# Two transformer blocks on 256 tokens: logits by quarters of rows, a put-off residual, a transferred pair of rows and cross-attention of raw rows

## The chip, the cores and the metric

One core of one Trainium2 chip. The metric is the device time of one execution in microseconds (us); a lower time is better. The core's engines work side by side: TensorE (PE, matrix products; its weight loads are shown as PEld), VectorE (DVE), ScalarE (ACT), GpSimd (POOL) and SyncE (SP), whose queue issues the stream of weights.

## The reference

x has 256 rows of 1024 columns, in f32. Block one, once:

```
h = rms_norm(x, g_mix);  z = h @ w_in           # q, k, v, su, sv, two gates
x += (sig(ga) * (attention(q, k, v) @ w_att_out) + sig(gb) * (sgu(su, sv) @ w_sgu_out)) @ w_out
x += cross_attention(rms_norm(x, g_cross), rms_norm(mem, g_mem))   # 4 heads of 128
x += moe(rms_norm(x, g_moe))       # best of 4 groups, then top 2 of its 4 experts
x  = rms_norm(x, g_final)
```

In cross-attention the scores are softmax(q k^T / sqrt(128)) with q = h @ w_cq, and w_ckv gives keys and values of the normed memory; then @ w_co. The MoE has 16 experts of (silu(t Wg) * (t Wu)) Wd with 512 hidden columns.

Block two, twice (the mixer is stick-breaking attention, then retention), with shift, scale and gate from c:

```
x = layer_norm(sqrt(2) * x + (1 + gate) * mixer(x * (1 + scale) + shift))
x = layer_norm(sqrt(2) * x + (1 + gate) * moe2(x * (1 + scale2) + shift2))
```

Stick-breaking attention takes log(1 - sigmoid(z)) under a causal mask, its suffix sums, and weighs values with exp(log sigmoid(z) + suffix), masked. moe2 is the same kind of MoE; its groups are ranked by the sum of the two best softmax values.

## The kernel before

x lies in SBUF as two tiles of 128 rows (t = 0, 1) side by side, each of two halves of 512 columns (n = 0, 1). All weights, about 440 MB, come through SP's queue in units of 1 MB in the order of use (`Stream`, lines 97 to 207), into a ring of 22 units (RING) in 24 tiles. Dense stages split each unit into a high part (ACT, line 172) and the rest (DVE, line 173) and multiply in three products (lines 423 to 425 and 441 to 443). A planner orders each engine's instructions by program order and estimated costs; what is wrapped in `keep_in_program_order` ("pin") stays in program order.

Block one (`block1`, from line 501) ends with cross-attention. `denseT` makes ck, the keys (line 696), then `T` turns m, the merged branches, by sixteen PE transposes (line 354; ACT line 372 and DVE line 373 evict), and the output product updates x (line 705). `normed` (line 330) makes xn, x times its rows' norm factor; the products of the values cv are the filler `fill`, two steps of which run before the transposes of xn (c) and the product cq. `xscores` makes scores for each head and calls `softmax` (lines 471 to 487: maximum, Exp with the row sums, reciprocal, and two ACT copies, line 486, that divide). `probT` (line 495) transposes, and line 751 multiplies with the values.

Each MoE (`moe`, from line 976) begins with a prelude: sixteen transposes of x, evicted with the scale sc into Y by eight operations of 128x256 (lines 361 and 363); the norm's factors; warming matmuls (`warm`, line 384, products of constants that nobody reads; the WARM tuples give their numbers for the three MoEs); products with the router's weights (line 1010), a copy (line 1014) and a product that adds four partial sums (line 1016); the normed rows xs (lines 1020 to 1024); the logits lg (line 1028); `route`, a chain of small DVE operations whose result sl lets PE compute places (line 1041); more warming; then the dispatch products px (line 1188). Seven rounds follow (`ROUNDS`), each for the slots of 2 to 4 experts: gate products pg, up products pu, down products py (line 1066, 7 us each). `down` splits the weighed results (lines 1103 to 1108) and adds them to x through the placing products pc (`put`, lines 1117, 1118, 1120): the first half of the columns at once, the second half, put(1), after a `yield`, which the next round resumes once its gate products stand:

```
late = down(hid, downs, wsl[:, p % 2 : p % 2 + 1], PT, tiles(p == LAST), p, p == LAST)
next(late, None)
if p in (XP - 1, LAST):
    self.do(late)
```

XP = 4, so after the fourth round put(1) is done at once, and then comes a branch (`extras`, line 1359) around a loop for tokens that no slot took. With even p a product pw (line 1203) brings the slot weights of two rounds.

In the third MoE the gain and bias of the last norm (four rows of 512) are fetched by POOL (`gains`), and in the sixth round (HOOK = 5) `rows` spreads them over the partitions by eight products (`spread`, line 1498) with four ACT copies. `last_norm` (line 1452) has three quarters on DVE and one on ACT and POOL, then the output's four transfers. In `stick`, POOL multiplies sp with a triangle of ones (line 1568) ahead of z's products (line 1576).

## Time and profile before

| what | value |
|---|---|
| runs | 1292.48, 1294.85, 1300.04 us; median 1294.85 |
| profiled execution | 1298.88 us, of it the span 1297.3 |
| mean granted TensorE clock | 0.979 of full speed |
| busy | PE 1214.7 us, DVE 729.5, ACT 404.6, POOL 126.8 |
| moved | 445.08 MB, mean 343 GB/s |

The span reaches from the first to the last instruction. [...] Block one lasts to 240 us, its MoE to 459, stick-breaking attention to 602, the second MoE to 832, retention to 1051, the third MoE to 1286. In a timeline line, "[2.21 <-DVE m L373]" says that the engine was idle for 2.21 us before this instruction, and what released it; "x16" joins sixteen neighbours.

### The profile page before, as it was taken

How to read it: one execution, taken by the hardware profiler on the slowest of the kernel's cores; microseconds unless marked ns; L12 is line 12 of the kernel's file. 1: busy time of each engine (PE TensorE's matmuls, PEld its weight loads, DVE VectorE, ACT ScalarE, POOL GpSimd, SP SyncE). 2: the span in 40 equal slices, each digit the busy share in tenths (PEclk: the TensorE clock that was granted, in tenths of full speed). 3: DMA queues.
4: the chain of work that ended last, by engine and by line, in shares of the span. 5: the costliest groups of instructions: out<-in, count | busy, mean ns of one | idle time of the engine just before them, and what ended most of it. 6: DMA issues, size and time to landing. Idle time of an engine off the chain costs nothing. (4 is left out here: it accounts for less than half of the span.)

```text
span 1297.3 us, 18613 instructions
## 1 busy us (share of the span) xinstructions
PE 1214.7 (94%) x6985; PEld 767.9 (59%) x6985; DVE 729.5 (56%) x1621; ACT 404.6 (31%) x695; POOL 126.8 (10%) x136
## 2 busy tenths in 40 slices
PE   6999988999999889999999899799999999998995
PEld 5877867644434378876443344488888874433442
DVE  5999986622222189976633222579898653332225
ACT  5776536310000144663100001243346431000011
POOL 1000200000000021332000000230102000000101
PEclk9999998999999989999999999999999989999998
DMA  9976867699999998787799999958798577999991
GB/s 366 407 271 257 307 284 297 255 410 421 421 419 422 418 421 311 280 312 274 283 420 421 420 420 419 421 215 297 265 330 341 185 301 293 419 420 421 419 416 44
DMA packets 64352, 445.08 MB, mean 343 GB/s; under 512 B 7364, under 2 KB 7876, under 8 KB 11904
## 3 DMA queue, kind: packets, MB, share of 16 engines
q1 hardware_dynamic: 62352, 439.91, 85.1%
q10 hardware_dynamic: 1296, 2.61, 0.5%
q8 instruction: 57, 0.93, 0.3%
q0 software_dynamic: 608, 1.32, 0.3%
q14 instruction: 39, 0.32, 0.1%
HBM read 442.75 MB, written 1.05 MB: 342 GB/s over the span
## 5 line engine op out<-in xcount | busy, mean ns | idle before, releaser
L173 DVE TENSOR_TENSOR hl<-w,hl 128x1024 fp32r<-128x1024 f32 (+1 forms) x154 | 191.3, 1254 | 53.4 <-ACT hl L172 52.9
L172 ACT CAST hl<-w 128x1024 fp32r<-128x1024 f32 (+1 forms) x160 | 165.3, 1040 | 172.1 <-PE dn L425 93.9
L1066 PE MATMUL pg<-w,XT 128*64 128x512 f32 (+1 forms) x864 | 162.8, 599 | 0.0
L1066 PE MATMUL py<-w,hid 128*64 128x512 f32 (+2 forms) x912 | 155.7, 573 | 3.0 <-ACT hid L1080 3.0
L1066 PE MATMUL pu<-w,XT 128*64 128x512 f32 (+1 forms) x864 | 155.8, 603 | 0.0
L1405 DVE TENSOR_TENSOR hid<-hid,pu 128x512 f32<-128x512 f32 x21 | 14.4, 687 | 179.0 <-PE pu L1066 179.0
L1120 DVE TENSOR_TENSOR x<-x,pc 128x512 f32<-128x512 f32 (+1 forms) x90 | 54.8, 648 | 89.3 <-PE pc L1118 88.7
L1066 PEld LDWEIGHTS pu<-w,XT 128*64 128x64 f32 (+1 forms) x864 | 47.0, 126 | 95.6 <-issue 93.3
L1066 PEld LDWEIGHTS py<-w,hid 128*64 128x64 f32 (+1 forms) x912 | 48.8, 125 | 91.9 <-issue 82.3
L1066 PEld LDWEIGHTS pg<-w,XT 128*64 128x64 f32 (+1 forms) x864 | 47.3, 126 | 91.7 <-issue 90.3
L829 DVE CUSTOM_DVE_ANT_0 w<-w,scr,vec 128x512 f32<-128x512 f32 x96 | 73.0, 790 | 0.0
L829 DVE CUSTOM_DVE_ANT_0 w<-w,scr,adaT 128x512 f32<-128x512 f32 x96 | 72.7, 792 | 0.0
L1054 PE MATMUL px<-O,xs 128*128 128x128 f32 x576 | 70.5, 276 | 0.0
L1054 PEld LDWEIGHTS px<-O,xs 128*128 128x128 f32 x576 | 67.1, 192 | 2.5 <-issue 2.5
L1391 ACT ACTIVATE hid<-pg 128x512 f32<-128x512 f32 x21 | 12.6, 599 | 159.9 <-PE pg L1066 159.9
L1107 ACT CAST yh<-y 128x512 fp32r<-128x512 f32 x26 | 16.1, 620 | 126.1 <-DVE y L1106 116.5
L1058 POOL TENSOR_TENSOR XT<-XT,adaT 128x512 f32<-128x512 f32 x24 | 25.0, 1042 | 286.7 <-DVE XT L1056 217.2
L1087 ACT CAST O<-pP 128x256 fp32r<-128x256 f32 x21 | 7.8, 373 | 143.1 <-PE pP L1086 134.0
L423 PE MATMUL dn<-hl,h 128*128 128x512 f32 (+1 forms) x128 | 49.5, 392 | 2.9 <-ACT hl L172 2.9
L423 PE MATMUL dn<-hl,e 128*128 128x512 f32 x128 | 51.0, 398 | 0.0
L1106 DVE SCALAR_TENSOR_TENSOR y<-py,ws,gate 128x512 f32<-128x512 f32 x26 | 19.5, 750 | 55.3 <-PE py L1066 55.2
L425 PE MATMUL dn<-hl,e 128*128 128x512 f32 x128 | 49.9, 390 | 0.0
(541 smaller groups left out, 2319.5 us busy)
## 6 DMA issues: line engine op xcount, KB each, us to landing
w<-e SPq DMA_DIRECT2D x282, 1024.0 KB, 13.4
w<-w SPq DMA_DIRECT2D x78, 1024.0 KB, 8.1
...
```

The source lines that it names most:

```text
L172: a = k.nc.scalar.copy(hi, w)
L173: b = eng.tensor_sub(lo, w, hi.bitcast(F32))
L423: nc.tensor.matmul(o, a, wh[:, c, :], start=(first and c == 0), stop=False)
L425: nc.tensor.matmul(o, b, wh[:, c, :], start=False, stop=(last and c == m - 1))
L829: pin(nc.vector.tensor_tensor_reduce(w[:, j, :], w[:, j, :], self.scr[:, u * 512 : (u + 1) * 512], 1.0, o if u else first, ALU.mult, ALU.a ...
L1054: nc.tensor.matmul(ps[:, c * P : (c + 1) * P], xs[:, t * D + (k0 + c) * P : t * D + (k0 + c + 1) * P], O[:, t * P : (t + 1) * P].bitcast(F ...
L1058: nc.gpsimd.tensor_add(xo, xo, sh_v[:, k0 : k0 + 4].unsqueeze(2).to_broadcast([P, 4, P]))
L1066: nc.tensor.matmul(out[a : a + w, :], lhs[:, a : a + w], ws[e][(slice(None), c, *h)], start=start, stop=stop, tile_position=(0, a))
L1106: nc.vector.scalar_tensor_tensor(y, py, w, gate[:, n * 512 : n * 512 + 512], ALU.mult, ALU.mult)
L1107: nc.scalar.copy(yh, y)
L1120: nc.vector.tensor_add(a, a, pc)
L1405: nc.vector.tensor_mul(hid[:], hid[:], pu[:])
```

## The change

The keys' products and the transposes of m alternate. Cross-attention transposes x itself; the norm's row factor, times 1/sqrt(128), goes as scale into the maximum and the Exp. `softmax` becomes `exps` and `shares`, all exps before the shares; in cross-attention DVE makes one half of the shares. In the MoEs the router's weights are multiplied by sc beforehand (on POOL for the first, in `offsets` for the others), the transposes are evicted by four plain ACT copies of 128x512, the products are done by quarters (a half of the contraction for one row tile), and the mean's part is added to the logits by an operation `dev`; xs is made inside `route` (`normed`), pinned. The numbers of warming matmuls change. The branch comes after the third round (XP = 3), and only the last round finishes put(1) at once. The last norm's rows come by `rows_load` on SP's queue, called in the last round. `last_norm` is all on DVE, pinned. In `stick` the triangle product becomes an `affine_select` on POOL. The diff, cut:

```diff
@@ -34,7 +34,7 @@
 ALPHA = float((2 * 2) ** 0.25)
-XP, NX = 4, 2
+XP, NX = 3, 2
@@ -42,13 +42,12 @@
 EARLY = 3
-HOOK = 5
-WARM_LOGITS, WARM_PLACES, WARM_INPUTS, WARM_AFTER = (4, 4, 4), (0, 4, 4), (4, 4, 4), (4, 4)
+WARM_LOGITS, WARM_PLACES, WARM_INPUTS, WARM_AFTER = (2, 2, 2), (2, 12, 12), (4, 4, 4), (20, 20)
@@ -468,22 +467,32 @@
-    def softmax(self, ps, scale, name):
-        nc = self.nc
-        s3 = ps[:].rearrange("p (a b) -> p a b", a=2)
+    def exps(self, ps, scale, name, rows=None):
+        nc = self.nc
         m = self.sm(name + "m", [P, 2])
-        nc.vector.tensor_reduce(m[:], s3, AX, ALU.max)
...
+        nc.vector.tensor_reduce(m[:], ps[:].rearrange("p (a b) -> p a b", a=2), AX, ALU.max)
+        if rows is None:
+            nc.vector.tensor_scalar(m[:], m[:], -scale, None, ALU.mult)
+        else:
+            nc.vector.scalar_tensor_tensor(m[:], m[:], -1.0, rows[:], ALU.mult, ALU.mult)
+        e, s = self.b2(name + "e"), self.sm(name + "s", [P, 2])
         for i in range(2):
-            nc.scalar.activation(e[:, i * 256 : (i + 1) * 256], ps[:, i * 256 : (i + 1) * 256], AF.Exp, bias=m[:, i : i + 1], scale=scale, accum_out=s[:, i : i + 1])
+            nc.scalar.activation(e[:, i * 256 : (i + 1) * 256], ps[:, i * 256 : (i + 1) * 256], AF.Exp, bias=m[:, i : i + 1], scale=scale if rows is None else rows[:, i : i + 1], accum_out=s[:, i : i + 1])
+        return e, s
+    def shares(self, e, s, name, engs):
+        nc = self.nc
             q = e[:, i * 256 : (i + 1) * 256]
-            nc.scalar.activation(q, q, AF.Copy, scale=r[:, i : i + 1])
+            if engs[i] == "v":
+                nc.vector.tensor_scalar(q, q, r[:, i : i + 1], None, ALU.mult)
+            else:
+                nc.scalar.activation(q, q, AF.Copy, scale=r[:, i : i + 1])
@@ -693,10 +703,14 @@
-        self.do(self.denseT(gH, gL, 2, ev_ck))
         m = sig[0]
-        mH, mL, _ = self.T(lambda t, k: m[:, t * D + k * P : t * D + (k + 1) * P], "m", 8, scale=0.5)
-        del aH, aL, sH, sL, sig, m
+        turn = self.trans(lambda t, k: m[:, t * D + k * P : t * D + (k + 1) * P], "m", 8, scale=0.5)
+        for i, _ in enumerate(self.denseT(gH, gL, 2, ev_ck)):
+            if i:
+                next(turn)
+        self.do(turn)
+        mH, mL, _ = self.out
+        del aH, aL, sH, sL, sig, m, turn
@@ -714,15 +728,15 @@
-        xn = self.normed(x, "xc", st)
         next(fill), next(fill)
-        cH, cL, _ = self.T(lambda t, k: xn[:, t * D + k * P : t * D + (k + 1) * P], "c", 8, scale=lambda k: self.vec(V_GCROSS + k))
-        del xn
+        cH, cL, _ = self.T(lambda t, k: x[:, t * D + k * P : t * D + (k + 1) * P], "c", 8, scale=lambda k: self.vec(V_GCROSS + k))
+        rc = self.rms(x, "xc", st)
+        nc.vector.tensor_scalar(rc[:], rc[:], float(128 ** -0.5), None, ALU.mult)
@@ -736,14 +750,14 @@
                 nc.tensor.matmul(s[:, qt * 256 : (qt + 1) * 256], cq[:, h, qt * P : (qt + 1) * P], ck[:, h, :], start=True, stop=True)
-            return self.softmax(s, float(128 ** -0.5), "c")
+            return self.exps(s, None, "c", rc)
         del gH, gL
-        pts = [self.probT(e, "cT") for e in es]
+        pts = [self.probT(self.shares(*e, "c", "av"), "cT") for e in es]
@@ -840,21 +854,24 @@
-    def row_load(self, r, out=None):
+    def row_load(self, r, out=None, eng=None):
         g = self.b4("rowl") if out is None else out
-        self.nc.scalar.dma_start(g[:], self.ap["rows"][r : r + 2].rearrange("a b -> (a b)").partition_broadcast(P))
+        (eng or self.nc.scalar).dma_start(g[:], self.ap["rows"][r : r + 2].rearrange("a b -> (a b)").partition_broadcast(P))
-    def rows_load(self, i):
+    def rows_load(self, i, eng=None):
         t = self.b8("rows")
-        return [self.row_load(r + 2 * i, t[:, o : o + D]) for o, r in ((0, R_LNG), (D, R_LNB))]
+        return [self.row_load(r + 2 * i, t[:, o : o + D], eng) for o, r in ((0, R_LNG), (D, R_LNB))]
-        self.wr = self.b2("wr", F32, (P, 256))
-        self.nc.scalar.dma_start(self.wr[:], self.ap["wr"][i])
+        self.wr = self.b2("wr")[:, :256]
+        self.nc.scalar.dma_start(self.wr, self.ap["wr"][i])
+        if i == 0:
+            w = self.wr.rearrange("p (k n) -> p k n", k=8)
+            self.nc.gpsimd.tensor_mul(w, w, self.vec(V_GMOE, 8).unsqueeze(2).to_broadcast([P, 8, 32]))
@@ -876,7 +893,8 @@
             nc.vector.tensor_reduce(sums[:], ps[:].rearrange("p (s k n) -> p s n k", s=2, k=8), AX, ALU.add)
-            self.ww = None
+            nc.vector.tensor_scalar(sums[:, 0], sums[:, 0], -1.0, None, ALU.mult)
+            self.wr, self.ww = self.ww[:, :256], None
@@ -920,6 +939,7 @@
             gl, el = lg[:, :, 0:4], lg[:, :, 4:20]
+            normed()
@@ -927,7 +947,8 @@
             nc.vector.tensor_sub(pr[:], el, bc(m, 16))
-            nc.scalar.activation(pr[:], pr[:], AF.Exp)
+            self.tc.keep_in_program_order(nc.scalar.activation(pr[:], pr[:], AF.Exp))
+            normed()
@@ -987,50 +1008,60 @@
-        tr = self.trans(lambda t, k: x[:, t * D + k * P : t * D + (k + 1) * P], "r", 8, scale=col(sc_v), parts=False, full=True, on_dve=(1, 3, 5, 7) if first else ())
-        next(tr), next(tr)
+        Y, wr, sums = self.b8("Y", F32, (P, 8, 256)), self.wr, self.sums
+        pl, pt, part = self.aux("lp"), self.aux("lg"), self.b2("lpart", F32, (P, 256))
+        def turned(h, t):
+            ps = self.aux("r")
+            for j in range(4):
+                k = 4 * h + j
+                nc.tensor.transpose(ps[:, j * P : (j + 1) * P], x[:, t * D + k * P : t * D + (k + 1) * P], self.ident)
+            pin(nc.scalar.copy(Y[:, 4 * h : 4 * h + 4, t * P : (t + 1) * P], ps[:].rearrange("p (j q) -> p j q", j=4)))
+        def products(h, t):
+            for j in range(4):
+                k = 4 * h + j
+                nc.tensor.matmul(pl[32 * j : 32 * j + 32, t * P : (t + 1) * P], wr[:, 32 * k : 32 * k + 32], Y[:, k, t * P : (t + 1) * P], start=(h == 0), stop=(h == 1), tile_position=(0, 32 * j))
+        turned(0, 0), turned(0, 1), turned(1, 0)
+        turned(1, 1)
             mu, rs = self.ln_factors(x, sx, "xn")
-        self.do(tr)
-        Y = self.out[2]
-        del tr
+        products(0, 0), products(1, 0), products(0, 1)
         self.warm(WARM_LOGITS[S.moes])
-        wr, sums = self.wr, self.sums
...
+        products(1, 1)
+        for t in range(2):
+            pin(nc.scalar.copy(part[:, t * P : (t + 1) * P], pl[:, t * P : (t + 1) * P]))
+            nc.tensor.matmul(pt[:, t * 32 : (t + 1) * 32], part[:, t * P : (t + 1) * P], self.cst(C_SELJ, 32), start=True, stop=True)
         self.wr = self.sums = None
-        part = self.b2("lpart", F32, (P, 256))
...
         xs = self.b8("xs")
-        if first:
...
+        lg, dev = self.sm("lg", [P, 2, 32]), self.sm("dev", [P, 2, 32])
             q = pt[:, t * 32 : (t + 1) * 32]
-            pin(nc.vector.scalar_tensor_tensor(lg[:, t], q, rs[:, t : t + 1], sums[:, 1] if first else add[:, t], ALU.mult, ALU.add))
+            if not first:
+                pin(nc.vector.scalar_tensor_tensor(dev[:, t], sums[:, 0], mu[:, t], q, ALU.mult, ALU.add))
+                q = dev[:, t]
+            pin(nc.vector.scalar_tensor_tensor(lg[:, t], q, rs[:, t : t + 1], sums[:, 1], ALU.mult, ALU.add))
+        def normed():
+            if first:
+                for t in (1, 0):
+                    pin(nc.scalar.activation(xs[:, t * D : (t + 1) * D], x[:, t * D : (t + 1) * D], AF.Copy, scale=rs[:, t : t + 1]))
+                return
+            off = self.sm("off", [P, 1])
+            pin(nc.vector.scalar_tensor_tensor(off[:], mu[:, 1], -1.0, rs[:, 1:2], ALU.mult, ALU.mult))
+            pin(nc.scalar.activation(xs[:, D:], x[:, D:], AF.Identity, bias=off[:], scale=rs[:, 1:2]))
+            pin(nc.vector.tensor_scalar(xs[:, :D], x[:, :D], mu[:, 0], rs[:, 0:1], ALU.subtract, ALU.mult))
         gate = None if first else row
-        r = self.route(lg, first)
+        r = self.route(lg, first, normed)
@@ -1213,7 +1244,7 @@
         if ahead is not None:
-            ahead(False)
+            ahead()
@@ -1391,10 +1422,8 @@
                 self.lnexp()
-            if p == HOOK and hook is not None:
+            if p == LAST and hook is not None:
                 hook()
-            if p == HOOK - 1 and hook is not None:
-                ahead(True)
@@ -1418,7 +1447,7 @@
             next(late, None)
-            if p in (XP - 1, LAST):
+            if p == LAST:
@@ -1452,21 +1481,21 @@
         nc = self.nc
+        pin = self.tc.keep_in_program_order
+        parts = [(t, slice(n * 512, (n + 1) * 512), x[:, t * D + n * 512 : t * D + (n + 1) * 512]) for n in range(2) for t in range(2)]
         mv = self.stats(x, "nl", st)
-        off = self.sm("nlo", [P, 1])
...
+        def less(t, c, o):
+            pin(nc.vector.scalar_tensor_tensor(o, o, mv[:, t, 0:1], g[:, c], ALU.subtract, ALU.mult))
+        va = self.sm("nlv", [P, 2])
+        pin(nc.vector.tensor_scalar(va[:], mv[:, :, 1], LN_EPS, None, ALU.add))
+        less(*parts[0])
+        rs = self.rsqrt(va[:], 2, "nl")
+        for i, (t, c, o) in enumerate(parts):
+            if i:
+                less(t, c, o)
+            pin(nc.vector.scalar_tensor_tensor(o, o, rs[:, t : t + 1], b[:, c], ALU.mult, ALU.add))
@@ -1565,7 +1594,7 @@
                 nc.vector.scalar_tensor_tensor(sp[:].rearrange("p a b -> p (a b)"), z[:, :384], 0.0, e[:], ALU.max, ALU.add)
-                nc.gpsimd.tensor_mul(sp[:, 0::2, :], sp[:, 0::2, :], tri.unsqueeze(1).to_broadcast([P, 2, P]))
+                nc.gpsimd.affine_select(sp[:, 0::2, :], sp[:, 0::2, :], [[0, 2], [1, P]], ALU.is_gt, 0.0, base=0, channel_multiplier=-1)
@@ -1881,8 +1910,8 @@
-            def ahead(last):
-                held["g"] = self.gains(3 if last else 2 * i)
+            def ahead():
+                held["g"] = self.gains(2 * i)
@@ -1890,13 +1919,7 @@
             def rows():
-                t = self.b8("rows")
...
+                held["r"] = self.rows_load(3, nc.sync)
```

## Rows read from the trace of the kernel before

**Rows 1.** The page: busy time, share of the span, instructions of each engine.
```profile
PE 1214.7 (94%) x6985; PEld 767.9 (59%) x6985; DVE 729.5 (56%) x1621; ACT 404.6 (31%) x695; POOL 126.8 (10%) x136
```

**Rows 2.** 10-us windows: busy us (instructions) of each engine, TensorE's clock, DMA share, GB/s.
```profile
190.00:200.00 10.00, 7.11 (x32) 5.53 (x32) 4.66 (x9) 3.29 (x6) 0.00 (x0) 0.72 0.00 0
...
740.00:750.00 10.00, 7.49 (x25) 2.94 (x26) 5.30 (x13) 0.62 (x1) 0.00 (x0) 0.83 1.01 415
...
1060.00:1070.00 10.00, 8.15 (x38) 7.38 (x37) 8.61 (x54) 3.62 (x8) 0.00 (x0) 0.66 0.39 162
...
1230.00:1240.00 10.00, 10.00 (x36) 4.09 (x34) 1.62 (x3) 2.66 (x5) 0.00 (x0) 0.83 1.01 420
```

**Rows 3.** PE's waits, 150 to 262 us: line, releaser, us in total, times, longest.
```profile
PE cT L495 <- ACT ce L486: 3.7, 3, 1.4
...
PE dn L425 <- DVE m L373: 2.2, 1, 2.2
```

**Rows 4.** Timeline 181 to 229 us: start, length, engine, line, operation, [idle before <- releaser].
```profile
181.07 0.68 DVE L705 TENSOR_TENSOR x<-x,dn 128x512 f32<-128x512 f32 x1
...
194.28 1.67 DVE L330 TENSOR_SCALAR xcn<-x,xc 128x512 f32<-128x512 f32 x4
...
228.34 0.58 PE L423 MATMUL dn<-hl,o 128*128 128x512 f32 x1
```

**Rows 5.** Timeline of the second MoE's prelude, 606 to 611 us.
```profile
606.59 0.16 DVE L287 TENSOR_TENSOR xn<-xn,xnt 128x2 f32<-128x2 f32 x1
...
607.64 1.24 ACT L1023 ACTIVATE xs<-x,off,xn 128x1024 f32<-128x1024 f32 x1
...
608.47 0.41 DVE L1028 SCALAR_TENSOR_TENSOR lg<-lg,xn,add 128x32 f32<-128x32 f32 x2 [0.34 <-PE lg L1016]
...
610.28 0.18 DVE L933 TENSOR_TENSOR ps<-pr 128x16 f32<-128x16 f32 x1 [0.95 <-ACT pr L930]
```

**Rows 6.** Timeline: the first MoE's px (249 us), the third's selection and px (1062 us).
```profile
249.69 2.97 PE L1188 MATMUL px<-O,xs 128*128 128x128 f32 x24
...
1062.39 1.10 PE L1041 MATMUL pos<-sl,tri 128*128 128x16 f32 x5 [1.85 <-DVE sl L917]
...
1065.18 5.30 PE L1188 MATMUL px<-O,xs 128*128 128x128 f32 x28
```

**Rows 7.** Timeline after the first MoE, 466 us.
```profile
466.59 3.67 PE L354 MATMUL b<-cst,x 128*128 128x128 f32 x16 [5.52 <-DVE x L330]
```

**Rows 8.** Timeline at the branches of the second and third MoE.
```profile
740.90 0.74 PE L1118 MATMUL pc<-yl,O 128*128 128x512 f32 x2 [0.85 <-DVE yl L1108]
...
742.41 0.73 PE L1117 MATMUL pc<-yh,O 128*128 128x512 f32 x2 [0.78 <-ACTq L1359]
...
744.76 0.72 PE L1203 MATMUL pw<-cbr,O 128*128 128x32 f32 x4 [0.55 <-DVE x L1120]
...
1195.17 0.72 PE L1117 MATMUL pc<-yh,O 128*128 128x512 f32 x2 [1.55 <-ACTq L1359]
```

**Rows 9.** Line 1359: ns least/median/most, first and last start.
```profile
L1359 PEldq COMPARE_BRANCH  x3: 355/403/444, 371.8 to 1195.9; - x3
```

**Rows 10.** The chain that ended last: start, us, what; the sixth round's and a later pu.
```profile
1233.54 2.04 PE rows L1498 x8
1235.59 8.71 PE pu L1066 x32
...
1265.10 7.04 PE pu L1066 x32
```

**Rows 11.** PE's waits, 480 to 590 us.
```profile
PE z L1576 <- POOL sp L1568: 5.0, 6, 1.2
```

**Rows 12.** Lines 1568 and 1581: ns least/median/most.
```profile
L1568 POOL TENSOR_TENSOR sp<-sp,tri x16: 727/1162/1692, 509.5 to 585.9; 128x256 f32<-128x256 f32 x16
...
L1581 POOL TENSOR_SCALAR_AFFINE_SELECT a<-a x16: 408/408/1310, 514.8 to 588.8; 128x256 f32<-128x256 f32 x16
```

**Rows 13.** Timeline of the last norm, 1289 us.
```profile
1288.79 1.25 DVE L284 TENSOR_TENSOR nlt<-nl 128x2 f32<-128x2 f32 x1
```

50 lines of the change are left out of this document (5 added, 45 removed).

## The prediction

> **What bounds the kernel now.** I read the page's engine shares first: TensorE (PE) is busy 94% of the span [rows 1], so its time is the kernel's, and a gain must be either PE idle time that goes or PE work at a lower clock that goes. Next the 10-us windows of the stretches that the diff touches. They show both: in 190 to 200 us PE is busy 7.11 of 10 us at granted clock 0.72, with no byte moved by DMA; in 1060 to 1070 us 8.15 at clock 0.66 [rows 2]. [...] Then the views of waits and the timeline, which name what PE waited for. The other two windows [rows 2] lie in mixture-of-experts (MoE) rounds: DMA share 1.01 at 415 to 420 GB/s, so there the weights' stream is as full as it gets, though no wait of PE for weights stands among the waits that I use.
>
> The profiled execution took 1298.88 us (span 1297.3 and 1.58 around it); the runs shown have the median 1294.85, 4.0 lower, and reach 1300.04. The sum is made against 1298.88.
>
> **1. ck's products between the transposes of m.** PE waits 2.21 us (2.2 in the view) for the low part of m, because the sixteen transposes come after all of ck's products and DVE is busy elsewhere [rows 3]. Put between the products, the transposes start earlier by several microseconds and the wait has cover. Bounds: 0 if DVE still serves its queue first, -2.4 if what follows comes sooner too. I take -2.0.
>
> **2. Cross-attention of raw rows.** x is final at 181.07 + 0.68 = 181.75 us. The normed copy starts on DVE at 194.28, takes 1.67, and PE's transposes follow it; the output projection starts at 228.34 [rows 4]. So 12.5 us pass between the rows being there and their use; DVE's queue holds weight splitting ahead of the norm. The change transposes raw x, and puts the norm's factor into the softmax's scale, where it is needed only after the scores. What fills the 12.5 us now is the value projection's first half, cut up by waits and then at half clock [rows 2]. The gap doesn't vanish whole: PE has that filler to do, it only gets transposes and the query projection to run with it. From 190 to 200 the idle share is 10 - 7.11 = 2.9 us; the half clock costs (1 - 0.72) x 10 = 2.8. Then the probabilities' transposes wait 3.7 us in three pieces for ACT's shares [rows 3]; with the four exps ahead of all shares, and half the shares on DVE, one of the three can stay. That is 2.9 + 2.8 + 2.5 = 8.2, and about 1 for the DMA queue, which stood still for the freed tile. I take -9. Low end: only the norm's own 1.67 and about 1.3 of the waits, -3. High end: all 12.5 us and 1.5 of the waits, -14. Late next is DVE, with max, shares and splitting in one queue.
>
> **3. The MoE's logits by quarters, three times.** In the second MoE the norm's factor is ready at 606.59 + 0.16 = 606.75, but the logits start at 608.47: products of 256 columns begin only after eight scaled evictions, and the wide rescaling of x sits on DVE ahead of the logits. ps then waits 0.95 us for an Exp that queues behind a gate eviction on ACT [rows 5]. After the change the logits can be ready shortly after the factor: 608.47 - 606.75 = 1.7 of it can go, less two small DVE operations of about 0.2 each, plus up to 0.7 of Exp's queueing. -1.8 in the first two, -2.3 in the third (its gap is 2.2 by the same lines): -6. The moved rescaling comes to lie in the Exp's wait; it must end before the places, some 3 us later, and is 1.24 long [rows 5]. Bounds -7, and -2 if the late quarter's eviction chain is what ends last.
>
> **4. Warming matmuls.** In the third MoE PE waits 1.85 us for the selection, then 28 products px take 5.30 (189 ns each) where the first MoE's 24 take 2.97 (124 each) [rows 6]: 28 x 65 ns = 1.8 lost to half clock. Twelve warming matmuls instead of four fill the wait: 8 more at 2.04 / 8 = 0.255 us, the spacing of eight such matmuls further on [rows 10], are 2.0. I give the clock some seven in ten to hold then: 0.7 x 1.8 = -1.3. Bounds -2.2, and +0.8 if they run at half clock and hold up what follows. After the first MoE PE waits 5.52 us for the norm of x [rows 7], and as long again after the second; 16 more matmuls (16 x 0.255 = 4.1) lie inside. At the end of such a gap a few microseconds at half clock follow; I take -1 each, -2 (from -4, held both times, to +2, warming that delays the transposes).
>
> **5. The branch one round earlier, with the second half put off across it.** At the branch the residual's second half is finished with nothing beside it: in the second MoE waits of 0.85, 0.78 and a smaller one, then 0.55 for the slot weights, and 1.55 in the third [rows 8]. The rows of the first MoE repeat 0.78 and 0.55. Those sum to 1.35, 2.5 and 2.1; in the second MoE clock 0.83 in its window [rows 2] costs another 0.8 or so. 6.7 in all. Deferred, put(1) runs after the next round's gate products; what stays at the branch is the branch. PE's weight queue shows 0.40 us for one, under other work so far [rows 9]; bare, three of them are 1.2. I take 6.7 - 1.2 = -5.5; -8 if the clock stays up everywhere, -2 if the planner leaves the second half's splits where PE still waits for them.
> [...]
>
> **6. The last norm's rows by a transfer.** Eight matmuls over 2.04 us go from the sixth round, and the next products take 8.71 instead of 7.04 us [rows 10], at clock 0.83 in their window [rows 2]: -2.0 - 1.7 = -3.7. Four ACT copies go with them, and two POOL transfers of the gains. Added are two transfers of 512 KB on SP behind the weights; nothing waits for them until the last norm, some 30 us later. Bounds -4 and -2 (the low clock has another reason).
>
> **7. The mask of stick-breaking attention.** z's products wait 5.0 us in six pieces for POOL's product with the triangle [rows 11]; it takes 1.16 us at the median, the select that replaces it 0.41 for the same 128x256 [rows 12]. 0.75 x 6 = 4.5 at most; a wait that shortens may uncover DVE's part: -3.5 (0 to -5).
>
> **8. Last norm.** All on DVE, where POOL and ACT had a quarter. A product of 128x2 takes 1.25 us there now, while POOL works [rows 13], and stands in the chain of the norm's factor; the same kind of operation on 128x2 takes 0.16 in the MoE prelude [rows 5]. 1.1 of it goes, and DVE does two wide operations more, outside the factor's chain in part: I take -0.6 (-2 to +1). The softmax of the first attention only changes order: 0.
>
> **Sum:** -2.0 - 9 - 6 - 1.3 - 2 - 5.5 - 3.7 - 3.5 - 0.6 = -33.6; 1298.88 - 33.6 = 1265.3. The best ends together give -48.6 (1250), the poor ends -5.2 (1294). Counted from the median the sum would be 1261; I say 1266, on the safe side of 1265.
>
> **Rivals.**
> *A: the gains are hidden elsewhere.* DVE and ACT are tight from 150 to 230 us, so cross-attention ends at its poor end (-3), the mask's wait moves to DVE (0), the after-MoE warming gives 0, the branches -2: -2 - 3 - 6 - 1.3 - 2 - 3.7 - 0.6 = -18.6, 1280. For it: the transposes' waits are already on ACT [rows 3]. Against it: the 12.5 us [rows 4] are one long gap with both engines below full.
> *B: the weights' stream takes over.* DMA share is 1.01 in the rounds [rows 2]; a faster PE may meet it. Then parts 3, 5 and 6 (-6 - 5.5 - 3.7 = -15.2) are lost: 1265.3 + 15.2 = 1280.5. Against it: PE's waits name no DMA.
> *C: the change does not do what it says at the branch.* The put-off half needs its buffers across the branch and may be pulled ahead of it: +5.5, 1271.
> [...]
>
> **How the numbers follow.** Forecast 0.56 (its own range 1252 to 1277), A 0.22, B 0.10, C 0.08, D 0.04. Faster by over 0.5% (below 1288.4; about what a measurement of this kernel tells from no change) holds for the forecast, C and nearly nine in ten of A and B: 0.56 + 0.08 + 0.23 = 0.87. Within 0.5%: the rest of A and B and a little of D, 0.09. Slower 0.04. The range 1250 to 1284 holds all of the forecast's and C's 0.64 but a few hundredths, and half to two thirds of A and B: 0.8.
>
> **What would show it.** Cross-attention: transposes of x by 188, output projection by 214 to 220, DMA at work between 190 and 200. MoE preludes: logits within 0.6 us of the norm's factor. After a branch: gate products within 1 to 2 us of the last down product, put(1) behind them. No rows matmul, and pu at 7.0. z's waits for POOL below 1.5 in sum. Wrong: a wait of PE for weights in the rounds; clock below 0.9 after the branches; an end near 1280 with cross-attention hardly moved.

## The result, and the profile after

| | before | after |
|---|---|---|
| median | 1296.03 us (four runs beside those of after; 1292.48 to 1300.04) | 1259.26 us (four runs; 1258.18 to 1261.16) |
| profiled execution: span | 1297.3 us | 1256.6 us |
| mean granted TensorE clock | 0.979 | 0.991 |

The ratio of the times is 0.9717, with a 95% interval from 0.9685 to 0.9749: the kernel is 2.8% faster. 1266 us was forecast, with a range from 1250 to 1284. The time came out in part by luck: by the sum of terms 33.6 us were to go and 40.7 went, with misses in both directions.

To see where the 40.7 us of span went, I took the start times of the same PE steps in both timelines and subtracted. The places leave little between them, since PE ends one stage where it begins the next:

| place | after minus before, us | forecast, us |
|---|---|---|
| up to the end of block one's mixer | -0.6 | 0 |
| ck and the transposes of m (part 1) | -1.5 | -2.0 |
| cross-attention (part 2) | -5.4 | -9 |
| three MoE preludes (parts 3 and 4) | -1.04, -0.60, -2.87 | -6 - 1.3 |
| first MoE, first pg to its pu | +0.75 | 0 |
| gaps after the first and second MoE (part 4) | -0.7, -2.7 | -1, -1 |
| rounds around the branch (part 5) | -3.8, -7.2, -6.6 | -5.5 in all |
| hook in the third MoE (part 6) | -4.9 | -3.7 |
| stick-breaking attention (part 7) | -2.9 | -3.5 |
| last norm (part 8) | -0.5 | -0.6 |
| sum | -40.6 | -33.6 |

A prelude is read from its first transpose to the first product pg (13.15, 16.74 and 19.43 us before, 12.11, 16.14 and 16.56 after). In the first MoE that cut shifts work: before, 24 dispatch products px lie ahead of the first pg and 8 behind it, after it is 20 and 12. That is 0.44 of the +0.75 in the next row, and 0.25 is a wait of pw for DVE; read to its first pu, the first prelude gained 0.3. Cross-attention fell short of its forecast by 3.6 and the preludes by 2.8, the branch went 12.1 beyond its own, and the rest is near.

The page after, engines' busy time, beside [rows 1]: TensorE works 14.5 us less inside a span that is 40.7 shorter, with 84 more instructions, so most of the gain (26.2) is idle time, and part is work at the higher clock (mean 0.991 instead of 0.979).

```profile
PE 1200.2 (96%) x7069; PEld 768.6 (61%) x7069; DVE 720.6 (57%) x1620; ACT 398.9 (32%) x681; POOL 116.8 (9%) x130
```

Windows of after, columns as in [rows 2]: the query projection of cross-attention, its probabilities' transposes, the third MoE's prelude, the place just behind it, and the place where the hook's products were.

```profile
190.00:200.00 10.00, 8.95 (x71) 8.57 (x72) 8.26 (x20) 5.41 (x11) 0.00 (x0) 1.00 0.11 26
...
210.00:220.00 10.00, 6.33 (x30) 5.59 (x30) 3.69 (x16) 8.57 (x24) 0.00 (x0) 0.83 1.01 421
...
1034.20:1044.20 10.00, 8.71 (x53) 6.24 (x53) 9.02 (x56) 5.12 (x11) 0.00 (x0) 1.00 0.40 165
...
1050.00:1060.00 10.00, 10.00 (x36) 3.71 (x35) 5.24 (x8) 0.60 (x1) 0.00 (x0) 0.83 0.93 338
...
1200.00:1210.00 10.00, 10.00 (x66) 6.03 (x64) 2.50 (x4) 0.75 (x2) 1.75 (x2) 1.00 1.02 422
```

Where [rows 2] has 7.11 busy at clock 0.72 there is 8.95 at 1.00; the third prelude's 8.15 at 0.66 has become 8.71 at 1.00, each window beginning 9.0 us after the first transpose. In windows of 1 us the lower clock reads 0.50, which is called half clock here: before from 196 to 199 us, from 466 to 472 behind the gap after the first MoE and from 1063 to 1069 in the third prelude, after from 1054 to 1057. Cross-attention keeps a window at 0.83, with 3.7 us idle. Its 1.00 from 190 to 200 is not in every trace: of the ten traces with this cross-attention (after and nine experiments that don't touch it) five have 1.00 there and five 0.83, and the stretch from the value product to the output projection takes 42.8 to 43.0 us in the first five and 44.1 to 44.7 in the others. The row -5.4 is thus one of two values; the other is near -3.9. The window from 1050 has 0.83 as well and no idle time at all: products of four rows begin in it (1051.12 us), of which more below.

Cross-attention after, timeline, beside [rows 4]: x is final at 178.41 + 0.67 = 179.08, its transposes start at 183.37, the output projection at 220.90.

```profile
178.41 0.67 DVE L719 TENSOR_TENSOR x<-x,dn 128x512 f32<-128x512 f32 x1
...
183.37 1.03 PE L353 MATMUL c<-cst,x 128*128 128x128 f32 x8
...
220.90 0.58 PE L422 MATMUL dn<-hl,o 128*128 128x512 f32 x1
```

PE's waits after, 150 to 262 us, beside [rows 3]: the wait for m is gone, the probabilities' transposes wait as long as before, in one piece instead of three.

```profile
PE cT L504 <- ACT ce L495: 3.7, 1, 3.7
```

The second MoE's prelude after, timeline, beside [rows 5]. The factor is ready at 591.06 + 0.16 = 591.22, and the last logits end 1.77 later (2.13 before); then Exp (ACT, line 950) starts behind two evictions of the gate (line 909), where one stood ahead of it before. ps's own wait is 0.26 instead of 0.95 because DVE now does the rescaling xs in that time: from the last logits to ps it takes 1.50, before 1.40.

```profile
591.06 0.16 DVE L286 TENSOR_TENSOR xn<-xn,xnt 128x2 f32<-128x2 f32 x1
...
592.01 0.25 DVE L1045 SCALAR_TENSOR_TENSOR dev<-sums,xnm,lg 128x32 f32<-128x32 f32 x1 [0.79 <-PE lg L1037]
...
592.74 0.25 DVE L1047 SCALAR_TENSOR_TENSOR lg<-dev,xn,sums 128x32 f32<-128x32 f32 x1
...
593.65 0.69 ACT L909 ACTIVATE gate<-gate,cst 128x512 f32<-128x512 f32 x1 [0.20 <-PE gate L908]
...
594.24 0.22 ACT L950 ACTIVATE pr<-pr 128x32 f32<-128x32 f32 x1
...
594.49 0.18 DVE L954 TENSOR_TENSOR ps<-pr 128x16 f32<-128x16 f32 x1 [0.26 <-ACT pr L950]
```

and before, ACT:

```profile
609.44 0.69 ACT L891 ACTIVATE gate<-gate,cst 128x512 f32<-128x512 f32 x1 [0.56 <-PE gate L890]
610.02 0.22 ACT L930 ACTIVATE pr<-pr 128x32 f32<-128x32 f32 x1
```

The branch, two views. First the fourth round of the first MoE, PE's timeline, before:

```profile
348.46 2.05 PE L1054 MATMUL px<-O,xs 128*128 128x128 f32 x16
350.44 7.05 PE L1066 MATMUL pu<-w,XT 128*32 128x512 f32 x58
...
358.35 0.66 PE L1079 MATMUL ph<-cst,hid 128*128 128x128 f32 x4 [0.85 <-DVE hid L1405]
```

and after:

```profile
332.84 7.08 PE L1097 MATMUL pg<-w,XT 128*32 128x512 f32 x64 [1.61 <-DVE yl L1135]
339.85 0.50 PE L1148 MATMUL pc<-yh,O 128*128 128x512 f32 x1
...
340.99 7.07 PE L1097 MATMUL pu<-w,XT 128*32 128x512 f32 x64
...
348.27 1.95 PE L1085 MATMUL px<-O,xs 128*128 128x128 f32 x16
350.06 0.60 PE L1110 MATMUL ph<-cst,hid 128*128 128x128 f32 x4
350.49 1.95 PE L1085 MATMUL px<-O,xs 128*128 128x128 f32 x16
352.37 7.07 PE L1097 MATMUL py<-w,hid 128*32 128x512 f32 x64
```

Before, the round ahead of the branch had half of the next round's dispatch (px) in front of most of pu instead of behind it, so that ph then had nothing to cover its wait for the hidden rows. After, the same round is in order and no wait stands in it but that of its pg, at the new branch place: 1.61 for DVE's yl. In the second MoE:

```profile
PE pg L1097 <- DVE y L1137: 0.9, 1, 0.9
```

So the branch still has a wait, another one. The third MoE's is 0.9 too. By steps, for the three MoEs, in us:

| step (PE start to start) | before | after |
|---|---|---|
| round 3, py to the next pg | 8.59, 9.23, 9.58 | 11.22, 11.16, 11.24 (the branch lies here) |
| round 4, pg to pu | 9.57, 10.02, 9.97 | 8.15, 8.13, 8.12 |
| round 4, pu to py | 13.23 in each | 11.38 in each |
| round 4, py to the next pg | 12.93, 14.85, 14.33 (the branch lay here) | 8.48, 8.02, 8.48 |

The rest of the row -3.8, -7.2, -6.6 is put(1), 1.2 to 1.4 us that come behind the next pg instead of ahead of it.

Hook, stick and last norm after, beside [rows 10], [rows 11, 12] and [rows 13]. The timeline at the hook's old place has no product with the rows, and pu takes 7.09 us where [rows 10] has 8.71, with clock 1.00 from 1195 to 1205 us where [rows 2] has 0.83:

```profile
1197.02 7.09 PE L1097 MATMUL pu<-w,XT 128*64 128x512 f32 x32
```

PE's waits in stick-breaking attention, and the line of the select (ns least/median/most):

```profile
PE z L1605 <- POOL sp L1597: 2.4, 5, 0.8
```

```profile
L1597 POOL TENSOR_SCALAR_AFFINE_SELECT sp<-sp x16: 408/856/1392, 497.2 to 570.9; 128x256 f32<-128x256 f32 x16
```

Last norm, timeline: the small product that took 1.25 takes 0.15.

```profile
1247.33 0.15 DVE L283 TENSOR_TENSOR nlt<-nl 128x2 f32<-128x2 f32 x1
```

### The profile page after: what moved, and what is told of

Same layout as the page of the kernel before. It is cut to its first block, busy times and chain, and to the rows that moved or that the text cites. A ratio compares the mean times of both kernels' runs of the same rounds, so it can differ in the third digit from the quotient of the medians.

```text
span 1256.6 us, 18759 instructions
## 1 busy us (share of the span) xinstructions
PE 1200.2 (96%) x7069; PEld 768.6 (61%) x7069; DVE 720.6 (57%) x1620; ACT 398.9 (32%) x681; POOL 116.8 (9%) x130
## 4 chain that ended last, share of the span: by engine, by line
PE 52%; DVE 4%; DMA 1%; ACT 1%; issue 1%; POOL 1%; DVEq 0%; ACTq 0%
PE pg L1097 8%; PE pu L1097 8%; PE py L1097 8%; PE dn L422 4%; PE dn L424 4%; PE dn L423 4%; PE px L1085 3%; PE pc L1148 1%; DMA w<-w 1%; PE dt L440 1%; PE dt L441 1%; PE dt L442 1%; PE pc L1149 1%; PE z L1605 1%; PE ph L1110 1%
## 5 line engine op out<-in xcount | busy, mean ns | idle before, releaser
L1097 PE MATMUL pg<-w,XT 128*64 128x512 f32 (+1 forms) x864 | 156.4, 595 | 3.4 <-DVE y L1137 1.8
L1097 PE MATMUL py<-w,hid 128*64 128x512 f32 (+2 forms) x912 | 152.6, 573 | 1.4 <-ACT hid L1111 1.4
L1097 PE MATMUL pu<-w,XT 128*64 128x512 f32 (+1 forms) x864 | 152.3, 599 | 0.7 <-DMA w<-e 0.7
```

What stands on the lines that cost most here:

```text
L1097: nc.tensor.matmul(out[a : a + w, :], lhs[:, a : a + w], ws[e][(slice(None), c, *h)], start=start, stop=stop, tile_position=(0, a))
```

## The experiments

Each experiment is an edit of the kernel after, unless told otherwise; ratios are to the kernel before, measured in the same rounds. Theory and rivals stand in the expectations.

**e1_now: put(1) not put off.** The branch stays where after has it.

```diff
-            if p == LAST:
+            if p in (XP - 1, LAST):
                 self.do(late)
```

> The changed kernel with the branch still after the third round, but the residual's second half done at once there (no put-off across the branch). Theory: the put-off is what pays at the branches, so the time from the first down product before the branch to the next gate product returns to that of the kernel before at its branch (12.9, 14.8, 14.3 us, against 11.2, 11.2, 10.8 in the changed kernel), and the round before the branch is again out of order; the span rises by 8 to 16 us over the changed kernel's 1256.6. Rival: the branch's place, after the third round instead of the fourth, is what pays; then the span stays within 3 us of 1256.6.

Measured: 1266.69 us (1264.54 to 1268.72), ratio 0.976 [0.9729, 0.9792]. In the profiles the branches lose 2.7, 3.0 and 2.6 against after, 8.3 in all; py to the next pg is 12.50, 13.58 and 13.60. The waits of [rows 8] are back, here in the second MoE:

```profile
PE pc L1148 <- ACTq L1390: 1.6, 1, 1.6
PE pc L1148 <- ACT yh L1138: 0.8, 1, 0.8
```

The rounds stay in order, which was not expected. In the first MoE 1.7 of the 2.7 is a wait of pg for "issue" behind the branch, of the kind told at the end. So putting off is worth 8.3 us where it now stands, 6.6 without that wait, and the rest of the 17.6 has to come from the branch's place.

**e2_rot: a fourth PSUM tile taken inside the branch.** Four tiles "mm" take turns; the branch takes three of them, and the pg behind it comes upon the tile whose second half is still to be split.

```diff
-                    px=self.aux("px"), pw=self.aux("pw"), pg=self.mm("pg"), pu=self.mm("pu"), py=self.mm("py"))
+                    px=self.aux("px"), pw=self.aux("pw"), pg=self.mm("pg"), pu=self.mm("pu"), py=self.mm("py"), pn=self.mm("pn"))
```

> The changed kernel with one more PSUM tile taken inside the branch (four instead of three of the pool of four), so that the next round's gate products get the tile after the one that they get now. Theory: what PE waits for after a branch (1.6, 0.9 and 0.9 us, for VectorE's split of the last down product) is the turn of the PSUM tiles: the gate products get the tile that the second half's down product still holds. With the extra tile these waits go and the span falls by 3 to 5 us. Rival: the branch itself costs it; then the waits stay under another name and the span stays within 1 us of 1256.6.

Measured: 1259.5 us, ratio 0.970 [0.9672, 0.9728]. The waits are the same 1.6, 0.9 and 0.9. As tested, the idea fell. Counting the turns, the branch's fourth tile is then itself the one that is waited for, and the wait stands where it stood; the next experiment tests that reading.

**e5_auxpy: the branch's py from the other four PSUM tiles.** The same idea with a turn less instead of one more.

```diff
-                    px=self.aux("px"), pw=self.aux("pw"), pg=self.mm("pg"), pu=self.mm("pu"), py=self.mm("py"))
+                    px=self.aux("px"), pw=self.aux("pw"), pg=self.mm("pg"), pu=self.mm("pu"), py=self.aux("py"))
```

> The changed kernel with the branch's own down product in a PSUM tile of the other pool, so that the branch takes two tiles of the first pool instead of three, and the gate products after it get the tile of the first down product, not of the second. In e2 the extra tile was one that the branch uses too, and the gate products still waited for VectorE. Theory (turn of the PSUM tiles): the waits of 1.6, 0.9 and 0.9 us after the branches go, and from the first down product to the next gate product it takes 9.3 to 10.3 us instead of 11.2, 11.2 and 10.8; span down by 2 to 4. Rival: the branch itself holds PE; then the waits stay within 0.4 under another name.

Measured: 1258.77 us, ratio 0.9712 [0.9682, 0.9741]. PE's wait at the first branch is now that for the branch alone:

```profile
PE pg L1097 <- PEq L1390: 0.3, 1, 0.3
```

py to the next pg is 9.95, 10.57 and 10.65: -1.27, -0.59 and -0.59. That shows what the new wait was: the turn of a PSUM tile. The whole did not move, and the first MoE says why for its part: its -1.14 before the fourth round has become -0.02 at its end, where this kernel, like after, waits for the stream:

```profile
PE pu L1097 <- DMA w<-e: 0.7, 1, 0.7
```

Before and e1_now have no such wait in the first MoE. What is gained there beyond after's rounds, the weights take back. In the third MoE's last round pu takes 7.74 here where it takes 7.09 after, both at clock 1.00, which points to the weights again,

```profile
1224.45 7.74 PE L1097 MATMUL pu<-w,XT 128*64 128x512 f32 x32
```

and in e4_vv, below, the same pu has a wait for weights that the view names.

**e6_xp4now: the branch back after the fourth round, put(1) at once.** All the rest of the change stays.

```diff
-XP, NX = 3, 2
+XP, NX = 4, 2
...
-            if p == LAST:
+            if p in (XP - 1, LAST):
```

> The changed kernel with the branch after the fourth round and the residual done at once there, as in the kernel before; all else changed. With e1 it separates the branch's place. Theory: with the branch there, the fourth round is laid out with the dispatch products px ahead of the up products, so that nothing is left to cover the last steps (up to down products 13.2 us instead of 11.4, gate to up 9.6 to 10 instead of 8.1), and the span is 8 to 10 us over e1's 1263.9. Rival: that layout came from other parts of the kernel before; then the span stays within 3 us of e1's.

Measured: 1281.3 us (1279.52 to 1282.04), ratio 0.988 [0.9849, 0.9911]: 14.6 above e1_now, where 8 to 10 was expected. Against after the branches' rounds lose 4.0, 8.9 and 9.3, 22.2 in all, and the wait in the gap after the second MoE about 4, of which the stage behind it makes up nearly half. The fourth round is again as it was before, with ph bare:

```profile
352.52 0.66 PE L1110 MATMUL ph<-cst,hid 128*128 128x128 f32 x4 [0.85 <-DVE hid L1434]
```

With e1_now's 8.3 for the putting off, the place is worth 22.2 - 8.3 = 13.9 here, and 17.6 - 8.3 = 9.3 measured from the kernel before. The fourth case, the branch after the fourth round with put(1) put off, was not run, so how far the two depend on each other is not shown. That the round ahead of a branch is put out of order when it is the fourth, and stays in order when it is the third, is what both timelines show; why the planner orders it so was not followed.

**e3_normed: cross-attention of normed rows again**, with the new order of exps and shares.

```diff
-        cH, cL, _ = self.T(lambda t, k: x[:, t * D + k * P : t * D + (k + 1) * P], "c", 8, scale=lambda k: self.vec(V_GCROSS + k))
-        rc = self.rms(x, "xc", st)
-        nc.vector.tensor_scalar(rc[:], rc[:], float(128 ** -0.5), None, ALU.mult)
+        xn = self.normed(x, "xc", st)
+        cH, cL, _ = self.T(lambda t, k: xn[:, t * D + k * P : t * D + (k + 1) * P], "c", 8, scale=lambda k: self.vec(V_GCROSS + k))
...
-            return self.exps(s, None, "c", rc)
+            return self.exps(s, float(128 ** -0.5), "c")
```

> The changed kernel with cross-attention of normed rows again (x times the norm's factor made on VectorE, transposed, constant scale in the softmax); exps and shares keep the changed order. Theory: the raw rows are what shortened the stretch from the first value product to the output projection (48.3 us before, 43.0 changed): it returns to 47 or 48, with a wait of the transposes for the normed rows and half clock around it. Rival: the exps ahead of the shares did it; then the stretch stays below 44.

Measured: 1263.01 us, ratio 0.973 [0.9702, 0.9757]. From the value product to the output projection it takes 46.56 us; after 42.97, before 48.34. The transposes wait for the norm:

```profile
191.51 1.29 PE L353 MATMUL c<-cst,xcn 128*128 128x128 f32 x8 [2.88 <-DVE xcn L329]
```

The window from 190 to 200 us has clock 0.83 here. Against the traces of the changed cross-attention that have 0.83 there too (44.1 to 44.7) the raw rows are worth 1.9 to 2.5, against after 46.56 - 42.97 = 3.6; the order of exps and shares has 48.34 - 46.56 = 1.8.

**e4_vv: all shares on DVE** (run once).

```diff
-        pts = [self.probT(self.shares(*e, "c", "av"), "cT") for e in es]
+        pts = [self.probT(self.shares(*e, "c", "vv"), "cT") for e in es]
```

> The changed kernel with all shares of cross-attention on VectorE, none on ScalarE. Theory: ScalarE is the bound between the scores and the transposes of the probabilities (its eight exps, two copies and four shares stand in one row), so PE's wait of 3.7 us before these transposes falls by 1 to 1.7. Rival: VectorE's queue (reciprocals at 211.6 us, three microseconds after the first sums are ready) is the bound; then the wait stays at 3.7 or grows.

Measured: 1257.52 us. The wait is shorter by 1.4:

```profile
PE cT L504 <- DVE ce L493: 2.3, 1, 2.3
```

The output projection comes 42.72 us after the value product, 0.25 less than in after. But this trace had lost 0.85 before the change acts, in the window where after has clock 1.00:

```profile
190.00:200.00 10.00, 8.83 (x61) 8.62 (x62) 7.72 (x18) 5.16 (x12) 0.00 (x0) 0.83 0.03 4
```

From the last value products to the output projection it takes 12.24 instead of 13.34, and against the unchanged traces with 0.83 in that window the stretch is 1.3 to 2.0 shorter. So most of the 1.4 arrives. PE's waits from 1190 us on, in the third MoE:

```profile
PE pu L1097 <- DMA w<-e: 0.7, 1, 0.7
```

The last two rounds there are 2.6 us longer than in after, so the stream hides what is gained ahead of them.

**e7_logits: the old logits**, with the new numbers of warming products.

```diff
-        turned(0, 0), turned(0, 1), turned(1, 0)
-        turned(1, 1)
+        tr = self.trans(lambda t, k: x[:, t * D + k * P : t * D + (k + 1) * P], "r", 8, scale=col(sc_v), parts=False, full=True, on_dve=(1, 3, 5, 7) if first else ())
+        next(tr), next(tr)
...
-        products(0, 0), products(1, 0), products(0, 1)
-        products(1, 1)
+                nc.tensor.matmul(pl[32 * j : 32 * j + 32, :256], wr[:, 32 * k : 32 * k + 32], Y[:, k, :], start=(r == 0), stop=(r == 1), tile_position=(0, 32 * j))
...
-        def normed():
```

> The changed kernel with the MoE logits as in the kernel before (eight scaled evictions, products of 256 columns, the wide rescaling ahead of the logits); the numbers of warming matmuls stay changed. From the first transpose to the first gate product the preludes took 13.15, 16.74 and 19.44 us before and take 12.11, 16.13 and 16.56 changed. Theory: the logits are worth their 1.0 and 0.6 in the first two, and 1 in the third, where the rest is the clock that the twelve warming matmuls keep: 13.1, 16.7, 17.5. Rival: the warming did all of it: 12.2, 16.2, 16.6.

Measured: 1265.68 us, ratio 0.9766 [0.9736, 0.9796]. The preludes take 12.70, 18.32 and 17.65: 0.6, 2.2 and 1.1 more than after's, 3.9 in all (3.1 with the first read to its first pu, where it is 0.2 shorter than after's). The rest of the difference has another place. PE's waits at the third MoE's branch:

```profile
PE pg L1085 <- PEq L1378: 2.9, 1, 2.9
PE pg L1085 <- issue: 1.0, 1, 1.0
```

After has 0.9 for DVE there, and this trace has after's 1.6 and 0.9 at the two branches ahead of it. With the lower clock behind it (0.57 from 1136 to 1140 us) the stall makes 5.7 us of the profiled span, and nothing of the logits is near it; it is taken up at the end.

**e10_warmold: the old numbers of warming products** (run once).

```diff
-WARM_LOGITS, WARM_PLACES, WARM_INPUTS, WARM_AFTER = (2, 2, 2), (2, 12, 12), (4, 4, 4), (20, 20)
+WARM_LOGITS, WARM_PLACES, WARM_INPUTS, WARM_AFTER = (4, 4, 4), (0, 4, 4), (4, 4, 4), (4, 4)
```

> The changed kernel with the old numbers of warming matmuls (4, 4, 4 before the logits; 0, 4, 4 before the places; 4, 4 after the MoEs). Theory: the added ones keep the clock in the gaps, so half clock comes back after the first and the second MoE (2.7 us in the second) and in the third prelude (about 1.8), the second prelude within 0.5; 3 to 5 us in all. Rival: they only fill waits: the stages are within 0.5 us each and the total within 1.

Measured: 1270.49 us. The preludes take 12.54, 17.55 and 19.33: 0.4, 1.4 and 2.8 more, and the third is again at half clock in part:

```profile
1040.00:1050.00 10.00, 8.92 (x40) 7.63 (x41) 8.67 (x54) 4.36 (x9) 0.00 (x0) 0.66 0.25 105
```

The gap after the first MoE is 0.15 to 0.7 longer, the one after the second 0.3 to 0.9 *shorter*: in after the transposes there start only as the twenty products end. So the new numbers ahead of the logits and the places, which this run does not separate, earn some 4.6 in the three preludes, and warming after a MoE next to nothing. 5.3 us of the span are a stall like e7's, at the same branch, and 1.7 a longer stretch in the second MoE's first round; 3 to 5 in all were expected, and the span is 12.3 longer.

What took 2.7 from the gap after the second MoE, then? The timeline before, DVE and POOL in the norm there:

```profile
832.58 4.64 POOL L173 TENSOR_TENSOR hl<-w,hl 128x1024 fp32r<-128x1024 f32 x2 [4.44 <-ACT hl L172]
...
834.97 2.27 DVE L285 TENSOR_TENSOR n1t<-n1t,n1v 128x2 f32<-128x2 f32 x1
```

and after:

```profile
810.33 0.16 DVE L284 TENSOR_TENSOR n1t<-n1t,n1v 128x2 f32<-128x2 f32 x1
...
812.95 4.90 POOL L172 TENSOR_TENSOR hl<-w,hl 128x1024 fp32r<-128x1024 f32 x2 [7.87 <-DMA w<-w]
```

A DVE operation on two columns took 2.27 us beside POOL's split of weights and 0.16 without it. After, that split comes later, since its weights do. The rows show the two side by side: 2.27 is about one of the two POOL instructions (4.64 / 2), and both end together, at 837.24 and 837.22. What makes DVE's operation last as long as POOL's is not shown. The other traces have the two together as well: only before and e6_xp4now have the long operation (2.27 and 2.26, in e6_xp4now ending at 829.03 with POOL's split at 829.01), and in them PE's transposes start 8.4 us after the products ahead of the gap (scr) begin, in e10_warmold 4.7 and in the other eleven 6.2, just behind the twenty warming products. After the first MoE nothing changed: two such operations take 1.73 and 2.26 us in every trace, before and after, and the transposes start 8.3 after those products. The 0.7 that this gap lost lies in the transposes themselves (3.32 to 2.63 us), which take 2.0 to 3.5 in the traces with twenty warming products; that the warming did it is not shown.

**e8_spread: the last norm's rows by products again**, the gains fetched a round earlier (run once).

```diff
-            if p == LAST and hook is not None:
+            if p == 5 and hook is not None:
...
-                held["r"] = self.rows_load(3, nc.sync)
+                for j in range(4):
+                    ps = self.aux("rows")
+                    self.spread(ps, gains, j)
+                    nc.scalar.copy(t[:, j * 512 : (j + 1) * 512], ps[:])
```

> The changed kernel with the last norm's rows spread by eight products in the sixth round again, as before. Theory: 2.0 us of matmuls and about 1.7 us of half clock after them come back, and POOL's gains with them; with the residual no longer at a branch nothing else moves, so 3.7 to 4.9 more from the sixth round's gate products to its down products, clock 0.83 in the window after. Rival: the low clock had another reason: 2.0 more, clock 1.00.

Measured: 1263.23 us, +5.0 in the span. The products take 2.05, and pu behind them 8.78, against 7.09:

```profile
1200.35 8.78 PE L1097 MATMUL pu<-w,XT 128*64 128x512 f32 x32
```

```profile
1200.00:1210.00 10.00, 10.00 (x42) 3.55 (x41) 0.69 (x1) 1.48 (x4) 0.00 (x0) 0.83 1.01 420
```

2.05 + 1.69 of the 5.0 are the forecast's two terms of part 6; 1.3 had come up ahead of the place.

**e11_warm8: eight warming products in that place**, of 128 rows instead of four (run once).

```diff
+            if p == 5 and hook is not None:
+                self.warm(8)
```

> The changed kernel with eight warming matmuls (128 rows in the contraction, 512 columns) at the place in the sixth round of the third MoE where the kernel before spread the rows with eight products of 4 rows; the transfer stays. In e8 the spread cost 2.05 for itself, 1.7 of half clock after it and 1.3 of order before it. Theory: products that use 4 of the 128 rows make the clock fall; with 128 rows there is 1.9 to 2.0 in all and clock 1.00. Rival: any foreign matmuls there let it fall: 3.6 or more, clock 0.83 in one window.

Measured: 1260.24 us. They cost 1.75 in all, and no clock:

```profile
1197.24 1.91 PE L383 MATMUL warm<-tri 128*128 128x512 f32 x8
```

```profile
1200.00:1210.00 10.00, 10.00 (x65) 5.76 (x62) 1.81 (x3) 0.74 (x2) 0.80 (x1) 1.00 1.02 421
```

With e8_spread this speaks for the four rows, and against the rival that any products set in there bring the low clock. It is one trace, and four rows don't bring the low clock each time either (see the end), so it is not settled.

**e9_tri: POOL's product with the triangle again** (run once).

```diff
-                nc.gpsimd.affine_select(sp[:, 0::2, :], sp[:, 0::2, :], [[0, 2], [1, P]], ALU.is_gt, 0.0, base=0, channel_multiplier=-1)
+                nc.gpsimd.tensor_mul(sp[:, 0::2, :], sp[:, 0::2, :], self.tri[:, :P].bitcast(F32).unsqueeze(1).to_broadcast([P, 2, P]))
```

> The changed kernel with POOL's product with the triangle again in stick-breaking attention, in place of the select. Theory: the product's length (1.16 us at the median against 0.41) is what PE waited for: PE's waits for it come back, near 5 us in some six pieces, and the stage from its first transposes to the second MoE's first transposes takes 134.4 to 135.1 us instead of 131.5. Rival: the 2.9 us that the stage gained came from its start (warming and clock after the first MoE); then it takes 131.5 to 132.3.

Measured: 1260.84 us. From the stage's first transposes to the second MoE's it takes 133.57 us; after 131.51, before 135.11. The waits of [rows 11] are back to the tenth:

```profile
PE z L1605 <- POOL sp L1597: 5.0, 6, 1.3
```

The select is worth 2.1 by the whole stage, and 2.7 behind its first transposes, which take 0.6 longer in after's trace than in this one.

**e12_best: e5_auxpy and e4_vv together, with the gate's row issued behind the selection** (five rounds).

```diff
-        pts = [self.probT(self.shares(*e, "c", "av"), "cT") for e in es]
+        pts = [self.probT(self.shares(*e, "c", "vv"), "cT") for e in es]
...
-        row = self.gate_row((0, 1, 3)[S.moes])
-        gate = None if first else row
         r = self.route(lg, first, normed)
         sel = next(r)
+        row = self.gate_row((0, 1, 3)[S.moes])
+        gate = None if first else row
...
-                    px=self.aux("px"), pw=self.aux("pw"), pg=self.mm("pg"), pu=self.mm("pu"), py=self.mm("py"))
+                    px=self.aux("px"), pw=self.aux("pw"), pg=self.mm("pg"), pu=self.mm("pu"), py=self.aux("py"))
```

> The changed kernel with three edits together: the branch's down product in the other PSUM pool (e5), all shares of cross-attention on VectorE (e4), and in the MoE preludes the gate row issued after the routing, so that the Exp no longer queues behind its evictions on ScalarE. Theory: branches -1.3, -0.6, -0.6 as in e5 (the first given back to the weights' stream by the end of the first MoE), cross-attention -0.3, the second and third prelude -0.7 each, the first -0.2: about 2.5 less, ratio to the kernel before near 0.970. Rival: the gate's products, no longer in the gap before the places, hold up the first round instead: preludes the same or longer, total within 1 us of the changed kernel.

Measured: 1255.31 us (1253.26 to 1256.25), ratio 0.9682 [0.9656, 0.9707], beside before's 1295.43 in the same rounds. ACT in the second MoE's prelude:

```profile
590.23 0.69 ACT L909 ACTIVATE gate<-gate,cst 128x512 f32<-128x512 f32 x1 [1.53 <-PE gate L908]
590.94 0.23 ACT L950 ACTIVATE pr<-pr 128x32 f32<-128x32 f32 x1
...
592.20 0.67 ACT L909 ACTIVATE gate<-gate,cst 128x512 f32<-128x512 f32 x1
```

Exp now stands behind one eviction instead of two, and the second and third preludes are 0.36 and 0.72 shorter (the third takes 16.2 to 16.6 in the traces that leave it alone). The branches are as in e5_auxpy, cross-attention 1.0 shorter than in after (42.01; 2.1 to 2.7 against the traces that, like this one, have 0.83 from 190 to 200), and the first MoE gives about 1.1 of it back to the stream (again 0.7 at pu). Its median is 4 us below after's, and its highest time below after's lowest, though the two were not timed in the same rounds and the intervals of the two ratios overlap.

## Why the prediction was right, and where it was not

The time was right because the direction of every part was, and because two parts that were counted too high (by 3.6 and 2.8) are made up, and more, by one that was counted 12.1 too low. That the sum landed within 7 us is luck as far as these three go.

**The branch (part 5) is the term that was mis-sized: -17.6 instead of -5.5.** The mechanism forecast was there: waits of the second half that go when it is put off, measured at 8.3 (e1_now), or 6.6 without the wait for "issue" there, where [rows 8] gave 6.7 less 1.2. But the step "6.7 in all" priced only the waits between py and the next pg. The same round had lost time ahead of py as well: 1.4 to 1.9 between pg and pu and 1.85 between pu and py, in each MoE, in a round that was out of order: half of its dispatch products in front of most of pu, and ph bare for 0.85. How the rest of that time divides was not followed. No wait for it stood in the rows that I had chosen; the sum of waits was read, and not the round's length beside that of its neighbours. e6_xp4now brings it back with the place. What I expected to stay, "1.2 bare", was too little: the new place costs 2.63, 1.93 and 1.66 between py and pg, of which 1.27, 0.59 and 0.59 are the turn of the PSUM tile (e5_auxpy) that I had not looked for at all. The sign named for it, pg within 1 to 2 us of the last down product, did show (327.60 + 3.63 to 332.84: 1.6).

**Cross-attention (part 2): -5.4 instead of -9.** Raw rows work as described: transposes at 183.37 (forecast by 188), clock 1.00 from 190 to 200, and DMA moving there again, if only at a share of 0.11. The term of 2.8 for the half clock is not safe, though: the clock falls there in half of the traces with the same code, at a cost of some 1.5 us. But the output projection started at 220.90, later than the 214 to 220 I had named, and the step "one of the three can stay" failed: the wait of 3.7 stayed whole, as one piece, and the window from 210 to 220 us still has clock 0.83. The work around the transposes moved ahead by more than the projection did. Rival A had this point (ACT and DVE are tight there), with -3 for its size; e4_vv, which takes work off ACT, shortens the wait by 1.4 and the way to the projection by 1.1.

**The logits (part 3) and the places (part 4): -4.5 instead of -7.3.** The step that took off the 1.7 between the factor and the logits of the second MoE, less two small operations, did not hold: from the factor to the end of the last logits it was 2.13 and is 1.77. DVE waits 0.79 for PE's product lg after the factor is there, and then does four small operations (592.01 to 592.99) where two did. The sign I had named, logits within 0.6, did not show. What else is gained is 0.35 from an earlier factor; Exp, where "up to 0.7" was open, got a second eviction ahead of it, and e12_best shows that its place is worth 0.36 in this prelude. Taken one at a time against after, the old logits cost 3.9 (e7_logits) and the old warming 4.6 (e10_warmold), 8.5 one by one where both together gave 4.5; the old logits with the new warming are even slower than before in the second MoE (18.32 against 16.74). So their gains can't be added. The -1.3 for half clock in the third MoE was low: that window is at 1.00 now, and with the old numbers of warming products the prelude is 2.77 longer (e10_warmold).

**After the MoEs (part 4): the size of 2 came out as 3.4, for another reason.** With the old warming the gap after the second MoE is no longer than with the new. What went there is a DVE operation that takes 2.27 us beside POOL's split and 0.16 without it; part 8 had priced one of that kind in the last norm (1.25 against 0.16), and none was looked for here. That term was right by luck.

**Hook, stick, last norm, m.** Part 6: 2.05 and 1.69 as priced, the high bound of -4 passed by 0.9 through 1.2 that came with the surroundings. Part 7: -2.9 for -3.5, inside its bounds; the select takes 0.86 at the median, not the 0.41 of [rows 12], so that z still waits for it 2.4, above the 1.5 that I had named as the sign. Part 8 and part 1 are within 0.5 of theirs.

**The rivals.** *C* (the half is pulled ahead of the branch) did not happen: put(1) stands behind pg. *D*, the slower case at 0.04, in which the clock falls at bare places, is refuted by the mean of 0.991, above the 0.979 of before. *B* (the stream takes over) is near. At the end of the first MoE a wait of 0.7 for weights now decides, and both e5_auxpy and e12_best gave about 1.1 back to it; e1_now is 3.7 later than after at that MoE's last pg and only 1.4 at its last py. In the third MoE's last round after has next to no time to spare (by the landings in the traces some 0.2 us where it is least, before 11): e4_vv waits there for weights, and in e5_auxpy, e9_tri and e12_best pu takes 7.7 to 7.9 us instead of 7.09. So the gains just fit under the stream, and a faster PE alone would probably bring little more there. *A* is right for cross-attention in part, wrong for the branches by the most of all.

**What stays open.** Why the planner lays the fourth round out of order ahead of a branch; why three branches took 6.17, 5.57 and 0.96 us, with waits of PE behind them, and the others 0.34 to 0.44; and why the clock falls in cross-attention in half of the traces. Parts 1 and 8 were read from the timelines alone, no experiment took them back.
